# Two halves of a weight chunk in one PSUM bank in the mixers' products, and one eviction for both where nothing stands between them

## The chip, the cores and the metric

The kernel runs on one core of a Trainium2 chip. The time is the device time of one execution in microseconds; the runs are compared by their medians. The profile is of one execution, and names TensorE (PE, with its weight loads PEld), VectorE (DVE), ScalarE (ACT), GpSimd (POOL) and SyncE (SP, which issues most DMAs).

## The reference

It is one block with a gated delta mixer and 16 experts, and behind it a second block of two layers, all in float32 on 256 tokens of 1024 features. The change is in the second block only. Cut to what matters:

```python
def second_block(x, ...):
    for l in range(2):
        x = x + 0.5 * swiglu_ffn(rms_norm(x, g_ffn1[l]), w_up1[l], w_down1[l])
        h = rms_norm(x, g_mix[l])
        z = h @ w_in[l]            # lx, lg, q, k, v (1024 columns each), forget (16), gates (2048)
        xr = causal_depthwise_conv(z_lx, conv_w[l], conv_b[l])
        hr = rg_lru(xr, ...)       # gates by 128 x 128 blocks, then a scan along the tokens
        y_lru = (gelu(z_lg) * hr) @ w_lru_out[l]
        o = forgetting_attention(q, k, v, f_logit, ...)   # 16 heads of 64, q and k normed per head
        y_attn = o @ w_attn_out[l]
        m = gate_lru * y_lru + gate_attn * y_attn
        x = x + m @ w_o[l]
        x = x + 0.5 * swiglu_ffn(rms_norm(x, g_ffn2[l]), w_up2[l], w_down2[l])
    return x
```

## The kernel before

The first block takes the first half of the span. Behind it stands block2, with two layers of feed-forward, mixer, feed-forward. Features lie on the 128 partitions, the 256 tokens (T) along the rows, so that a product gives a tile of 128 x 256.

Products keep float32 accuracy: each operand is split into a high and a low part of a faster type, and three matmuls of 128 x 256 are summed for every 128 rows of the contraction (mm3, lines 235 to 237). With 8 such blocks a product is 24 matmuls. The activations are split once per norm (xh and xl, lines 248 and 249). Weights come in chunks of 128 x 2048: SyncE starts the DMA into a ring, ScalarE copies each half of the chunk into the high part (whi, line 222), VectorE subtracts for the low part (wlo, line 223). The function weights keeps two chunks split ahead, and there are four buffers each of whi and wlo. A chunk of the mixer feeds two products, one per half (u = 0, 1), or one per half of the tokens for v.

Each product goes into a PSUM bank of the pool "mm", which has three (bank, line 402); a bank holds 128 x 512 float32. Attention has its own banks, "s" (three) and "sm" (two).

The mixer (mix) runs four groups, g = 0 to 3, each a chunk of q, k, v and lx. queries evicts each q and k product by a multiplication with the norm's factor rstd (VectorE, line 527) and squares it on ScalarE (line 529); norms sums the squares with matmuls (line 537). values evicts v on ScalarE with the factor per token (line 551). recurrence evicts lx on VectorE (line 636), runs the short convolution (line 641) and appends two scans. Attention (lines 553 to 619) and the scans (line 651 and on) run in the background: they are generators in the list live, and project advances each of them by one step after a product (tick). The Tile scheduler then sets the final order on each engine. A scan's two matmuls share one "mm" bank, and each half is read by a tanh on ScalarE (line 653).

Behind the groups come four chunks of lg (line 681), the gates (their two products share a bank and have been evicted by one 128 x 512 operation, line 699), the two output branches (la, lines 710 to 722) and w_o: each of its eight products is added to x on VectorE (line 732), and after each the next norm takes its step (high part on ScalarE, low part xl on VectorE, square, sum on GpSimd). The norm's sums are then summed over partitions by one matmul (line 258).

Of the kernel before, what the change touches and what calls it, by code (L numbers as in the profile page):

```python
# [12 lines left out]
AF = mybir.ActivationFunctionType  # L13
ALU = mybir.AluOpType
AX = mybir.AxisListType
P = 128
# [145 lines left out]
def ks(t):  # L162
    return [t[:, k] for k in range(KD)]
# [6 lines left out]
class Kernel:  # L170
# [257 lines left out]
    def mix(self, l, x, norm):  # L428
        nc, d, wp, ps = self.nc, self.d, self.wp, self.ps
        with ExitStack() as es:  # L430
# [71 lines left out]
            def project(out, *args, f=self.proj):  # L502

                nonlocal rstd
                f(out, *args)
                if rstd is None:
                    rstd = finish()
                tick()

            live.append(tokens())  # L510
            tmp("gap", (P, GAP2))
# [6 lines left out]
            def queries(g):  # L518

                qk[g] = [tmp("qs", (P, 2, T), 1), tmp("kk", (P, 2, T), 1)]  # L520
                sqs = []
                for i, nm in enumerate(("w_q", "w_k")):
                    w = self.weights(nm, l * 4 + g)
                    for u in range(2):
                        pq = self.bank()
                        project(pq[:, :T], w, u, xh, xl)
                        nc.vector.tensor_mul(qk[g][i][:, u], pq[:, :T], rstd)  # L527
                        sqs.append(tmp("sq", (P, T), 4))
                        nc.scalar.activation(sqs[-1], qk[g][i][:, u], AF.Square)
                live.append(norms(sqs, g))  # L530
# [13 lines left out]
            def values(g):  # L544

                vt[g] = tmp("vt", (P, 2, T), 2)
                w = self.weights("w_v", l * 4 + g)
                for t in range(2):
                    pv = self.bank()
                    project(pv[:, :T], w, xh, xl, slice(t * P, (t + 1) * P), f=self.vproj)  # L550
                    nc.scalar.activation(vt[g][:, t], pv[:, :T], AF.Copy, scale=rc[:, t:t + 1])

# [71 lines left out]
            def recurrence(g):  # L624
# [3 lines left out]
                nc.sync.dma_start(wax, d["w_ax"][l * 4 + g])  # L628
                w = self.weights("w_lx", l * 4 + g)
                for u in range(2):  # L630
                    m = 2 * g + u
                    pq = self.bank()
                    project(pq[:, :T], w, u, xh, xl)
                    lx = tmp("lx", (P, T + 3), 2)
                    nc.gpsimd.memset(lx[:, :3], 0.0)
                    nc.vector.tensor_mul(lx[:, 3:], pq[:, :T], rstd)
                    cw = lambda j: self.c(f"conv_w{l}", j * KD + m)
# [38 lines left out]
            for g in range(4):  # L676
                w = self.weights("w_lg", l * 4 + g)
                for u in range(2):
                    pq = self.bank()
                    project(pq[:, :T], w, u, xh, xl)  # L680
                    nc.vector.tensor_mul(lg[:, 2 * g + u], pq[:, :T], rstd)
            for e in range(2):
# [9 lines left out]
            def gates(m):  # L692
# [4 lines left out]
                tg[m] = tmp("tg", (P, 2, T), TG)  # L697
                p2 = pq.rearrange("p (s n) -> p s n", s=2)
                nc.vector.tensor_mul(tg[m], p2, rstd[:, None, :].to_broadcast([P, 2, T]))
                for s in range(2):  # L700
# [25 lines left out]
            for c in range(4):  # L726
                w = self.weights("w_o", l * 4 + c)
                for u in range(2):
                    m = 2 * c + u
                    pq = self.bank()  # L730
                    self.proj(pq[:, :T], w, u, ks(mh), ks(ml))
                    nc.vector.tensor_add(x[:, m], pq[:, :T], x[:, m])
                    norm[2](m)
# [852 lines left out]
```

## Time and profile before

| | us |
|---|---|
| median of three runs | 2591.66 |
| the three runs | 2591.61, 2591.66, 2594.95 |
| the profiled execution | 2593.31 |
| its span | 2591.6 |
| TensorE busy | 2238.6 (86%) |
| VectorE busy | 1204.3 (46%) |
| ScalarE busy | 990.8 (38%) |
| GpSimd busy | 288.4 (11%) |
| mixer of layer 0 | about 1502 to 1778 |
| mixer of layer 1 | about 2137 to 2412 |

Times in a trace are counted from the start of the span. A row of the timeline gives an operation's start, its duration, its engine and line, the tile that it writes and those that it reads, and in square brackets how long its engine had been idle ahead of it and what ended that. Matmuls overlap in TensorE's pipe: their shown duration is longer than the distance of their starts, which is what counts in a row of them. VectorE and ScalarE begin an operation shortly before the one ahead is shown to end.

### The profile page before, as it was taken

The numbers are of one execution on the slowest core, as the hardware profiler recorded it, in microseconds if no ns is written. First come the engines' busy times: TensorE is split into PE (matmuls) and PEld (weight loads), VectorE is DVE, ScalarE is ACT, GpSimd is POOL, SyncE is SP. The second block draws the span as 40 slices with busy tenths as digits, with TensorE's granted clock in tenths as the row PEclk, the third lists the DMA queues.
The fourth block names the chain that finished last, engine by engine and source line by source line (L and its number), as shares of the span: only waits on it lengthen the run. The fifth ranks groups of instructions, "written<-read, shape, count | busy, mean of one in ns | idle before, by whom it ended". The sixth has DMA issues, their size and how long they took to land.

```text
span 2591.6 us, 40993 instructions
## 1 busy us (share of the span) xinstructions
PE 2238.6 (86%) x17204; PEld 1683.9 (65%) x17204; DVE 1204.3 (46%) x1924; ACT 990.8 (38%) x1619; POOL 288.4 (11%) x373
## 2 busy tenths in 40 slices
PE   7998997676677667666799999999999999999999
PEld 3666883111122111111189988999999998899999
DVE  4797751000000000000055679867566568986654
ACT  4674651000000000000055567645555556765553
POOL 2442000000000000000011121102111111111110
PEclk9999998878888887888789999999999999999999
DMA  6146259999999999999945543455555554345554
GB/s 256 69 176 212 82 232 384 430 431 429 431 430 430 430 431 429 431 429 431 429 181 196 195 145 135 161 188 188 196 195 184 193 204 146 123 163 196 185 193 144
DMA packets 75160, 681.24 MB, mean 263 GB/s; under 512 B 10080, under 2 KB 13792, under 8 KB 15072
## 3 DMA queue, kind: packets, MB, share of 16 engines
q1 hardware_dynamic: 71920, 677.48, 66.0%
q8 instruction: 135, 2.21, 0.3%
q10 hardware_dynamic: 3056, 1.15, 0.2%
q14 instruction: 49, 0.40, 0.0%
HBM read 677.47 MB, written 1.05 MB: 262 GB/s over the span
## 4 chain that ended last, share of the span: by engine, by line
PE 48%; DMA 35%; DVE 10%; ACT 4%; issue 2%; ACTq 0%; POOL 0%; SPq 0%; DVEq 0%; POOLq 0%
PE mm L235 13%; PE mm L236 13%; PE mm L237 13%; DMA arena<-e_down 10%; DMA arena<-e_up 7%; DMA arena<-e_gate 6%; DMA expert_ring<-e_gate 5%; DVE wlo L223 3%; DMA expert_ring<-e_down 3%; DMA ring<-e_up 1%; DMA ring<-e_down 1%; DMA early_zs<-w_mod 1%; DVE xr L641 1%; ACT whi L222 1%; DVE y L1128 1%
## 5 line engine op out<-in xcount | busy, mean ns | idle before, releaser
L223 DVE TENSOR_TENSOR wlo<-ring,whi 128x1024 fp32r<-128x1024 f32 x460 | 584.2, 1273 | 302.8 <-ACT whi L222 302.7
L222 ACT ACTIVATE whi<-ring 128x1024 fp32r<-128x1024 f32 x460 | 485.0, 1056 | 375.0 <-PE mm L236 334.3
L235 PE MATMUL mm<-xh,whi 128*128 128x256 f32 x2152 | 601.3, 280 | 10.6 <-DVE kk L527 7.1
L237 PE MATMUL mm<-xh,wlo 128*128 128x256 f32 x2152 | 599.4, 279 | 0.0
L236 PE MATMUL mm<-xl,whi 128*128 128x256 f32 x2152 | 598.1, 278 | 0.2
L235 PEld LDWEIGHTS mm<-xh,whi 128*128 128x128 f32 x2152 | 406.1, 189 | 15.5 <-issue 6.3
L237 PEld LDWEIGHTS mm<-xh,wlo 128*128 128x128 f32 x2152 | 405.9, 189 | 0.3
L236 PEld LDWEIGHTS mm<-xl,whi 128*128 128x128 f32 x2152 | 405.5, 188 | 0.9 <-DVE xl L249 0.6
L936 DVE TENSOR_TENSOR hid<-hid,u 128x512 f32<-128x512 f32 x16 | 11.0, 687 | 501.1 <-PE u L932 501.1
L235 PE MATMUL mm<-hh,whi 128*128 128x256 f32 x704 | 194.3, 276 | 0.0
L236 PE MATMUL mm<-hl,whi 128*128 128x256 f32 x704 | 194.3, 276 | 0.0
L237 PE MATMUL mm<-hh,wlo 128*128 128x256 f32 x704 | 194.3, 276 | 0.0
L932 PE MATMUL u<-arena,xs 128*32 128x512 f32 x608 | 108.3, 843 | 71.1 <-DMA arena<-e_up 71.1
L958 DVE COPY y<-x 128x512 f32<-128x512 f32 x16 | 11.1, 691 | 315.6 <-PE x L953 315.6
L236 PEld LDWEIGHTS mm<-hl,whi 128*128 128x128 f32 x704 | 132.2, 188 | 0.0
L235 PEld LDWEIGHTS mm<-hh,whi 128*128 128x128 f32 x704 | 132.2, 188 | 0.0
L237 PEld LDWEIGHTS mm<-hh,wlo 128*128 128x128 f32 x704 | 132.2, 188 | 0.0
L944 ACT ACTIVATE ht<-x 128x512 f32<-128x512 f32 x16 | 9.6, 597 | 304.4 <-PE x L942 304.4
L932 PEld LDWEIGHTS u<-arena,xs 128*32 128x32 f32 x608 | 19.7, 132 | 159.3 <-DMA arena<-e_up 123.0
L932 PE MATMUL g<-arena,xs 128*32 128x512 f32 x640 | 85.3, 660 | 40.3 <-DMA arena<-e_gate 40.3
L953 PE MATMUL d<-arena,ht 128*32 128x512 f32 x304 | 76.8, 787 | 48.9 <-DMA arena<-e_down 44.1
L957 ACT ACTIVATE y<-d 128x512 f32<-128x512 f32 x16 | 9.6, 597 | 279.9 <-PE d L953 279.9
(521 smaller groups left out, 3903.8 us busy)
## 6 DMA issues: line engine op xcount, KB each, us to landing
ring<-up SPq DMA_DIRECT2D x88, 1024.0 KB, 4.8
arena<-e_gate SPq DMA_DIRECT2D x40, 2048.0 KB, 34.4
arena<-e_up SPq DMA_DIRECT2D x38, 2048.0 KB, 35.1
arena<-e_down SPq DMA_DIRECT2D x38, 2048.0 KB, 34.2
ring<-down SPq DMA_DIRECT2D x44, 1024.0 KB, 4.8
expert_ring<-e_down SPq DMA_DIRECT2D x20, 2048.0 KB, 34.1
expert_ring<-e_up SPq DMA_DIRECT2D x19, 2048.0 KB, 34.1
expert_ring<-e_gate SPq DMA_DIRECT2D x18, 2048.0 KB, 34.0
```

The source lines that it names most:

```text
L222: nc.scalar.activation(hi, r, AF.Copy)
L223: nc.vector.tensor_sub(lo, r, hi.bitcast(F32))
L235: mm(out, ah, bh, start=start, stop=False)
L236: mm(out, ah, bl, start=False, stop=False)
L237: mm(out, al, bh, start=False, stop=stop)
L641: nc.vector.scalar_tensor_tensor(xr, lx[:, j:j + T], cw(j), xr, op0=ALU.mult, op1=ALU.add)
L932: nc.tensor.matmul(gu[s][32 * q:32 * q + 32], xs[:, k, ec], w[:, 512 * q:512 * q + 512], start=(k == 0), stop=(k == KD - 1))
L936: nc.vector.tensor_mul(hid, hid, gu[1])
L944: nc.scalar.activation(ht, xb, AF.Copy)
L953: nc.tensor.matmul(dn[n][32 * q:32 * q + 32], ht[:, i * P + 32 * q:i * P + 32 * q + 32], ws[q][:, o:o + 512], start=(i == 0), stop=(i == 3))
L958: nc.vector.tensor_copy(y[1], dn[1])
L1128: stt(yv[:, :, o], sv[:, :, i], cw(j), yv[:, :, o], op0=ALU.mult, op1=ALU.add)
```

## The change

The two products of a chunk go into the two halves of one "mm" bank. For q, k and lg one VectorE operation of 128 x 512 evicts both (scaled, with rstd broadcast over the halves), and for q and k one ScalarE operation squares both. For v, lx and w_o the halves share the bank, but each half is still evicted by an operation of its own. The gates had this form and now use the new function. The number of banks stays at three.

```diff
--- before.py
+++ after.py
@@ -507,6 +507,16 @@
                     rstd = finish()
                 tick()
 
+            def two(f, w):
+
+                pq = self.bank()
+                for u in range(2):
+                    f(pq[:, u * T:(u + 1) * T], w, u, xh, xl)
+                return pq
+
+            def scaled(out, pq):
+                nc.vector.tensor_mul(out, pq.rearrange("p (s n) -> p s n", s=2), rstd[:, None, :].to_broadcast([P, 2, T]))
+
             live.append(tokens())
             tmp("gap", (P, GAP2))
             hr, lg = big(0), big(1)
@@ -521,12 +531,11 @@
                 sqs = []
                 for i, nm in enumerate(("w_q", "w_k")):
                     w = self.weights(nm, l * 4 + g)
-                    for u in range(2):
-                        pq = self.bank()
-                        project(pq[:, :T], w, u, xh, xl)
-                        nc.vector.tensor_mul(qk[g][i][:, u], pq[:, :T], rstd)
-                        sqs.append(tmp("sq", (P, T), 4))
-                        nc.scalar.activation(sqs[-1], qk[g][i][:, u], AF.Square)
+                    pq = two(project, w)
+                    scaled(qk[g][i], pq)
+                    sq = tmp("sq", (P, 2, T), 2)
+                    nc.scalar.activation(sq, qk[g][i], AF.Square)
+                    sqs += [sq[:, u] for u in range(2)]
                 live.append(norms(sqs, g))
 
             def norms(sqs, g):
@@ -545,10 +554,11 @@
 
                 vt[g] = tmp("vt", (P, 2, T), 2)
                 w = self.weights("w_v", l * 4 + g)
+                pv = self.bank()
                 for t in range(2):
-                    pv = self.bank()
-                    project(pv[:, :T], w, xh, xl, slice(t * P, (t + 1) * P), f=self.vproj)
-                    nc.scalar.activation(vt[g][:, t], pv[:, :T], AF.Copy, scale=rc[:, t:t + 1])
+                    h = pv[:, t * T:(t + 1) * T]
+                    project(h, w, xh, xl, slice(t * P, (t + 1) * P), f=self.vproj)
+                    nc.scalar.activation(vt[g][:, t], h, AF.Copy, scale=rc[:, t:t + 1])
 
             def attention(g):
                 qz, kz = tmp("qz", (P, 4, T), 2), tmp("kz", (P, 4, T), 2)
@@ -627,13 +637,14 @@
                 wax = tmp("wax", (P, 512), 2)
                 nc.sync.dma_start(wax, d["w_ax"][l * 4 + g])
                 w = self.weights("w_lx", l * 4 + g)
+                pq = self.bank()
                 for u in range(2):
                     m = 2 * g + u
-                    pq = self.bank()
-                    project(pq[:, :T], w, u, xh, xl)
+                    h = pq[:, u * T:(u + 1) * T]
+                    project(h, w, u, xh, xl)
                     lx = tmp("lx", (P, T + 3), 2)
                     nc.gpsimd.memset(lx[:, :3], 0.0)
-                    nc.vector.tensor_mul(lx[:, 3:], pq[:, :T], rstd)
+                    nc.vector.tensor_mul(lx[:, 3:], h, rstd)
                     cw = lambda j: self.c(f"conv_w{l}", j * KD + m)
                     xr = lr[0][:, u]
                     nc.scalar.activation(xr, lx[:, 0:T], AF.Identity, bias=self.c(f"conv_b{l}", m), scale=cw(0))
@@ -675,10 +686,7 @@
             other = self.aside(xh, xl)
             for g in range(4):
                 w = self.weights("w_lg", l * 4 + g)
-                for u in range(2):
-                    pq = self.bank()
-                    project(pq[:, :T], w, u, xh, xl)
-                    nc.vector.tensor_mul(lg[:, 2 * g + u], pq[:, :T], rstd)
+                scaled(lg[:, 2 * g:2 * g + 2], two(project, w))
             for e in range(2):
                 r = slice(4 * e, 4 * e + 4)
                 nc.scalar.activation(lg[:, r], lg[:, r], AF.Gelu_apprx_tanh)
@@ -695,8 +703,7 @@
                 for s in range(2):
                     project(pq[:, s * T:(s + 1) * T], w, s, *((xh, xl) if m or s else other))
                 tg[m] = tmp("tg", (P, 2, T), TG)
-                p2 = pq.rearrange("p (s n) -> p s n", s=2)
-                nc.vector.tensor_mul(tg[m], p2, rstd[:, None, :].to_broadcast([P, 2, T]))
+                scaled(tg[m], pq)
                 for s in range(2):
                     nc.scalar.activation(tg[m][:, s], tg[m][:, s], AF.Tanh, scale=0.5,
                                          bias=hb[:, 8 * s + m:8 * s + m + 1])
@@ -725,11 +732,12 @@
             norm = self.norm(x, f"g_ffn2{l}")
             for c in range(4):
                 w = self.weights("w_o", l * 4 + c)
+                pq = self.bank()
                 for u in range(2):
                     m = 2 * c + u
-                    pq = self.bank()
-                    self.proj(pq[:, :T], w, u, ks(mh), ks(ml))
-                    nc.vector.tensor_add(x[:, m], pq[:, :T], x[:, m])
+                    h = pq[:, u * T:(u + 1) * T]
+                    self.proj(h, w, u, ks(mh), ks(ml))
+                    nc.vector.tensor_add(x[:, m], h, x[:, m])
                     norm[2](m)
             return norm
```

The scheduler tracks a bank as a whole, so the order around these products moves too. In the rows below an instruction's line stands first, then its operation, what it writes and reads, and the semaphores of the engines for which it waits; mm_ with a number is one PSUM bank's tile, whi and wlo are weight halves, xh and xl the split activations. The lines of the changed kernel are 8 to 11 further down for the same statements (651 becomes 662, 751 becomes 759, 610 becomes 620).

The first place is TensorE in group 2, where the first half of k ends and the second begins, with a matmul of the scan (line 651) between them. Before:

```order
L236 MATMUL mm_9558<-xl_7901,whi_9446 128x256
L237 MATMUL mm_9558<-xh_7900,wlo_9447 128x256
L651 MATMUL mm_9583<-xr_9322,wax_9325 128x256 [waits DVE_49]
L235 MATMUL mm_9601<-xh_7900,whi_9450 128x256 [waits DVE_49]
L236 MATMUL mm_9601<-xl_7901,whi_9450 128x256
```

After:

```order
L236 MATMUL mm_9534<-xl_7901,whi_9426 128x256
L237 MATMUL mm_9534<-xh_7900,wlo_9427 128x256
L662 MATMUL mm_9559<-xr_9303,wax_9306 128x256 [waits DVE_49,PE_49]
L235 MATMUL mm_9534<-xh_7900,whi_9430 128x256
L236 MATMUL mm_9534<-xl_7901,whi_9430 128x256
```

The second half of k had a bank of its own, for which it waited for VectorE; now it goes on in the bank of the first half and waits for nothing.

The second place is TensorE in group 1, at the scan's last matmul (line 651, into a bank that a tanh reads). Before, it stands in the second half of k:

```order
L235 MATMUL mm_9179<-xh_7900,whi_9028 128x256
L236 MATMUL mm_9179<-xl_7901,whi_9028 128x256
L651 MATMUL mm_9161<-xr_8919,wax_8922 128x256 [waits Activation_49]
L237 MATMUL mm_9179<-xh_7900,wlo_9029 128x256
L235 MATMUL mm_9179<-xh_7900,whi_9028 128x256
```

After, it stands behind the transposes of the attention (line 620) and the first matmul of v (line 759):

```order
L620 MATMUL sm_9192<-pack_base,p_1226_9000 128x128 [waits DVE_49]
L620 MATMUL sm_9192<-pack_base,p_1226_9000 128x128
L759 MATMUL mm_9212<-whi_9114,xh_7900 128x256 [waits Activation_49]
L662 MATMUL mm_9147<-xr_8910,wax_8913 128x256 [waits Activation_49]
L760 MATMUL mm_9212<-wlo_9115,xh_7900 128x256
```

Ten matmuls of k and the six transposes have moved ahead of it. In groups 2 and 3 the same pair of places is found after, while before it stood between transposes or in k.

The third place is TensorE in w_o of layer 0, at the end of the first half of its first chunk; b_ are the two parts of the mixed branches. Before, the second half follows at once in another bank:

```order
L237 MATMUL mm_11694<-b_1486_10647,wlo_11618 128x256
L235 MATMUL mm_11694<-b_1486_10647,whi_11617 128x256 [waits Activation_49]
L236 MATMUL mm_11694<-b_1487_10648,whi_11617 128x256 [waits DVE_49]
L237 MATMUL mm_11694<-b_1486_10647,wlo_11618 128x256
L235 MATMUL mm_11723<-b_1486_10647,whi_11621 128x256
L236 MATMUL mm_11723<-b_1487_10648,whi_11621 128x256
```

After:

```order
L235 MATMUL mm_11646<-b_1458_10599,whi_11569 128x256 [waits Activation_49]
L236 MATMUL mm_11646<-b_1459_10600,whi_11569 128x256 [waits DVE_49]
L237 MATMUL mm_11646<-b_1458_10599,wlo_11570 128x256
L235 MATMUL mm_11715<-b_1458_10599,whi_11638 128x256
L236 MATMUL mm_11715<-b_1459_10600,whi_11638 128x256
L237 MATMUL mm_11715<-b_1458_10599,wlo_11639 128x256
L235 MATMUL mm_11715<-b_1458_10599,whi_11638 128x256
L236 MATMUL mm_11715<-b_1459_10600,whi_11638 128x256
L235 MATMUL mm_11646<-b_1458_10599,whi_11573 128x256 [waits DVE_49]
L236 MATMUL mm_11646<-b_1459_10600,whi_11573 128x256
```

Five matmuls of the second chunk (mm_11715) now stand between the halves of the first, whose second half waits for VectorE. Further on the same is done with seven matmuls of the next chunk ahead of each second half.

## Rows read from the trace of the kernel before

**Rows 1.** The page: TensorE's busy time; the chain that ended last, by engine.

```profile
PE 2238.6 (86%) x17204; PEld 1683.9 (65%) x17204; DVE 1204.3 (46%) x1924; ACT 990.8 (38%) x1619; POOL 288.4 (11%) x373
PE 48%; DMA 35%; DVE 10%; ACT 4%; issue 2%; ACTq 0%; POOL 0%; SPq 0%; DVEq 0%; POOLq 0%
```

**Rows 2.** Stretches: length, busy PE, PEld, DVE, ACT, POOL, then clock, DMA share, GB/s.

```profile
1545.00:1578.00 33.00, 32.09 (x265) 30.05 (x264) 32.28 (x62) 23.34 (x50) 5.96 (x11) 1.00 0.41 139
...
1664.00:1752.00 88.00, 87.81 (x774) 87.58 (x773) 60.70 (x67) 44.76 (x58) 8.70 (x10) 1.00 0.55 192
```

**Rows 3.** TensorE's waits, 1502 to 1778: us in total, times, longest.

```profile
PE mm L235 <- DVE kk L527: 3.5, 2, 2.6
PE ss L258 <- POOL sums L253: 1.3, 2, 0.9
PE mm L235 <- ACT ti L653: 0.9, 1, 0.9
...
PE mm L651 <- DVE qs L527: 0.4, 1, 0.4
```

**Rows 4.** Timeline of TensorE in w_o: two matmuls in a row.

```profile
1753.08 0.28 PE L235 MATMUL mm<-b,whi 128*128 128x256 f32 x1
1753.19 0.28 PE L236 MATMUL mm<-b,whi 128*128 128x256 f32 x1
```

**Rows 5.** Two lines' durations: ns min/median/max, first and last start, forms.

```profile
L527 DVE TENSOR_TENSOR kk<-mm,rstd x16: 404/419/425, 1514.5 to 2249.7; 128x256 f32<-128x256 f32 x16
...
L699 DVE TENSOR_TENSOR tg<-mm,rstd x16: 677/692/692, 1668.0 to 2367.5; 128x512 f32<-128x512 f32 x16
```

**Rows 6.** Timeline in group 1: a matmul into a bank being read.

```profile
1540.17 0.48 ACT L653 ACTIVATE th<-mm,hb 128x256 f32<-128x256 f32 x1
...
1540.70 0.30 PEld L651 LDWEIGHTS mm<-xr,wax 128*128 128x128 f32 x2 [0.16 <-ACT th L653]
```

**Rows 7.** Timeline in group 3: TensorE's longest wait in the mixer.

```profile
1608.13 2.35 DVE L223 TENSOR_TENSOR wlo<-ring,whi 128x1024 fp32r<-128x1024 f32 x2
...
1610.40 0.41 DVE L527 TENSOR_TENSOR kk<-mm,rstd 128x256 f32<-128x256 f32 x1
...
1610.96 0.36 PE L235 MATMUL mm<-xh,whi 128*128 128x256 f32 x1 [2.57 <-DVE kk L527]
```

**Rows 8.** Timeline of TensorE: where group cycles begin, and one wait.

```profile
1548.19 0.36 PE L751 MATMUL mm<-whi,xh 128*128 128x256 f32 x1
...
1575.49 0.60 PE L651 MATMUL mm<-xr,wax 128*128 128x256 f32 x2
1577.00 0.38 PE L235 MATMUL mm<-xh,whi 128*128 128x256 f32 x1 [0.91 <-DVE kk L527]
...
1580.86 0.36 PE L751 MATMUL mm<-whi,xh 128*128 128x256 f32 x1
...
1615.41 0.36 PE L751 MATMUL mm<-whi,xh 128*128 128x256 f32 x1
...
1648.05 0.37 PE L235 MATMUL mm<-xh,whi 128*128 128x256 f32 x1
```

**Rows 9.** Timeline in group 1: the scan's last matmul; the next low halves.

```profile
1545.99 0.42 PE L651 MATMUL mm<-xr,wax 128*128 128x256 f32 x1
...
1557.48 2.28 DVE L223 TENSOR_TENSOR wlo<-ring,whi 128x1024 fp32r<-128x1024 f32 x2
```

**Rows 10.** Timeline of ScalarE at the mixer's start: issues of DMAs.

```profile
1518.81 2.52 ACTq L563 DMA_DIRECT2D qz<-cum  x4
```

**Rows 11.** Timeline of ScalarE and VectorE in w_o, one turn.

```profile
1755.55 1.06 ACT L222 ACTIVATE whi<-ring 128x1024 fp32r<-128x1024 f32 x1 [0.66 <-PE mm L236]
...
1756.64 1.22 DVE L223 TENSOR_TENSOR wlo<-ring,whi 128x1024 fp32r<-128x1024 f32 x1 [0.56 <-ACT whi L222]
...
1757.79 0.96 DVE L249 SCALAR_TENSOR_TENSOR xl<-x,pack_base,xh 128x256 fp32r<-128x256 f32 x1
...
1758.67 0.41 DVE L732 TENSOR_TENSOR x<-mm,x 128x256 f32<-128x256 f32 x1
```

## The prediction, made before the changed kernel was run

> **What bounds the kernel now.** I read the page's busy table and its chain of waits first, then busy time by stretches, then what TensorE waited for, then the timeline around each wait. The busy table and the chain [rows 1] show TensorE busy for 86% of the span, and the chain split between TensorE (48%) and DMA (35%). The DMA part is the expert weights of the first block, which the change does not touch. The change sits in the mixer of the second block, which runs twice: about 1502 to 1778 us and 2137 to 2412 us, with the same pattern both times. So every sum below is for one mixer and is doubled at the end.
>
> Inside a mixer the reader is to see two kinds of stretch [rows 2]. In the four groups (queries, values, recurrence, with attention in the background) TensorE is busy 32.09 of 33 us, but VectorE too, 32.28 of 33. Here the two engines run neck and neck. Behind the groups (gates, output branches) TensorE is busy 87.81 of 88 us and VectorE 60.70: TensorE alone sets the pace. A product is 24 matmuls at a pitch of 0.113 us (1753.08 to 1753.19) [rows 4], 2.72 us, and 96 of them take 10.85 us.
>
> What TensorE waited for in the whole mixer is little [rows 3]: 3.5 us for evictions of k (two waits, one of 2.6), 0.9 for ti (a tanh that reads a bank of the recurrence), 0.4 for q, 1.3 for the norm's sums. But for the last these are waits for one of the three "mm" banks to come free. The largest of them is plain in the timeline [rows 7]: a pair of weight splits holds VectorE from 1608.13, the eviction of k starts behind it at 1610.40, and TensorE starts the next product at 1610.96, 2.57 us late. The starts of the values of groups 1 to 3 and of the first product behind them [rows 8] give group cycles of 32.67, 34.55 and 32.64 us, 99.86 together. In the first one the pair at 1575.49 is followed only at 1577.00; its second matmul starts at 1575.71, and where nothing is late the next one follows 0.03 behind, so 1.26 is lost. A cycle without bank waits is thus 32.67 - 1.26 = 31.4 us. All bank waits of the three cycles are 99.86 - 94.2 = 5.7 us: that is the most that the change can win there.
>
> **Part 1: one eviction for two products (q, k, lg).** An eviction of 128x256 takes 0.41 us, one of 128x512 takes 0.69 (the gates' own, which has this very form) [rows 5]. So two become one, 2 x 0.41 - 0.69 = 0.13 us less on VectorE, 12 times in a mixer: 1.6 us of VectorE time. Behind the groups this is hidden under TensorE; it counts in the group cycles only, as slack. What counts is that the second half of a chunk now writes the bank that the first half already holds: it needs no free bank, so the wait of [rows 7] has no place there any more. The price is that the first half's eviction now waits for the second half.
>
> **Part 2: the group cycles.** To the 31.4 I add three things. First, 0.2: the scheduler now cuts v, lx and the next q into pieces that alternate with the attention's matmuls in other places, with one more change of operand type. Second, 0.15: the second half of v and of lx writes the bank that the first half's eviction reads. The trace has such a case: the pair at L651 goes into a bank that a tanh reads until 1540.65, and its weight load, 0.16 idle for that tanh, starts at 1540.70, 0.05 behind its end [rows 6]. For v the order puts 19 matmuls of lx between the halves, for lx 14 of the next q, so only a part is left. Third, the next group's q needs its low weight half. The order puts the last matmul of the recurrence's scan behind the first one of v; before, in group 1, it came earlier, in k, at 1545.99. The low half of the next q began at 1557.48 on VectorE as one of two that take 2.28 together [rows 9], so it was ready at 1558.62, 12.6 us later, long before q came at its old place behind lx. Now q's first 14 matmuls stand ahead of the second half of lx, and between the scan's last matmul and q's third are 23 of v, 19 of lx, 24 of v, 5 of lx and 2 of q: 73 at 0.113, 8.25 us. The rest of a cycle, 31.4 less eight products of 2.72, is 9.6 us of attention and scan matmuls; a good quarter of them lies between, 2.6 by my estimate: 10.85 us. I take 11.5 for the chain: 12.6 less the eviction of k and its square (0.41 + 0.40), which now come ahead of it, and 0.3 for the queueing between them, an estimate. That leaves a wait of 0.65 us per cycle; its bounds are 0 (the chain is done in 10.85) and 2.0 (12.6 and 0.28 for the longer eviction in front). The sum is 31.4 + 0.2 + 0.15 + 0.65 = 32.4 per cycle, 97.2 for three, against 99.86: **2.7 us won**, with bounds from 4.8 won (31.7 per cycle, most of the 0.15 hidden, no wait) to 1.4 lost (33.75).
>
> **Part 3: the mixer's start.** On ScalarE the one square of k (128x512) now stands behind four DMA issues, which held the queue 2.52 us in the trace [rows 10], and behind a split, and the table load of the norms stands behind it again. The norms' matmuls come later for it, and v's second half waits for the first's eviction behind them on ScalarE: some 2.4 us in all. The old waits in group 1 (0.9 for ti, 0.4 for q [rows 3], and the steps around them, 1.9 in all against the pitch) go with it: a start that is later meets VectorE and ScalarE further on. So I set 2.4 against 1.9, and **0.5 us is lost**, between 0 and the whole 2.4.
>
> **Part 4: w_o.** Its halves share a bank but are still added to x one by one. VectorE's order is a fixed triple there, split, xl, add; the trace shows one turn of it [rows 11]: ScalarE's split from 1755.55 for 1.06, VectorE's from 1756.64 for 1.22, xl from 1757.79 for 0.96, add from 1758.67 to 1759.08. The product before had ended at 1755.40 (ScalarE's split waited for TensorE, by its row, and started 0.15 behind). So an add ends 3.7 us after the end of the product before its own, and TensorE can go on then. Before the change nobody waited for it: the next product had its own bank. Now the second half of a chunk waits. The scheduler puts 7 matmuls of the next chunk ahead of it: from the end of the product before, TensorE has 19 + 7 = 26 matmuls, 2.95 us, less the 0.15 by which it had begun: 2.8. The wait is 3.7 - 2.8 = 0.9 us for each of chunks 1 to 3, 2.7 together. Chunk 0 adds 0.1 (five matmuls, 0.57, ahead of an eviction of 0.41 and two handovers), and the next block's norm sum adds 0.4, since 18 matmuls cover it now instead of 22. **3.2 us lost.** The bounds: 0.5 if the xl takes 0.48 (as it does when POOL is still) and the scheduler's cover holds, so that only the last two terms are left, and 4.4 if another eviction of 0.41 stands in front each time.
>
> A page speaks against the change. The Trainium skill, "Perfetto Trace Analysis", section "Matmuls", says that independent matmul groups should go round different PSUM banks, so that the evacuation of one runs beside the matmuls of the next. This trace agrees in one place only [rows 6]; how far it bears on the halves is the third rival's matter.
>
> **The sum.** Per mixer 0.5 - 2.7 + 3.2 = +1.0 us, for two +2.0. The profiled execution took 2593.3 us (span 2591.6, and 1.7 around it), which becomes 2595.3; it stands 1.65 above the median of three runs, 2591.66. On the median's scale I predict **2593.7 us**. With a measurement that can tell about 0.2%, 5.2 us, from no change, this is no change.
>
> **The rivals.**
> - The cover is enough everywhere: cycles of 31.7 (4.8 won), w_o at its low bound (0.5), the start free. That is 4.3 won per mixer, 2583.1 us. For it: the scheduler did put cover in each place, and VectorE has 1.6 us more slack. Against: VectorE's 32.28 of 33 us, and the fixed triple of w_o. Chance 0.15.
> - Slower: the split queue comes late. One mechanism, in the group cycles: the low half of the next q's weights, behind the scan on VectorE. From 12.6 us after the scan's second half on, instead of my 11.5, the wait is 2.0 and the cycles 33.75, 1.4 lost; with 0.5 and 3.2 this is 5.1 per mixer, 2601.9 us. For it: VectorE is full there and the chain did take 12.6 before. Against: it has less in it now. Chance 0.18.
> - The halves are serialised through their bank: every second half of v, lx and w_o, 12 in a mixer, waits for the whole eviction of the first: 0.28 for the last matmul to end, 0.42 to 0.48 for the eviction and 0.08 of handovers, less the 0.11 of a pitch, 0.7 each, 8.2 in all. With the bank waits gone (and part of the rest hidden) 4.0 are lost per mixer, 2599.8 us. This is the result that the page's rule leads to. Against: the order has background or other products' matmuls between halves in most places. Chance 0.03.
> - The change does not do what it says: the bank waits stay, because VectorE is late and not the banks short. Then nothing of the 2.7 is won, the lost 0.5 and 3.2 remain, 3.7 per mixer, 2599.1 us. Against: in [rows 7] the eviction comes late, and a second half that needs no bank would have passed it. Chance 0.07.
>
> **How the numbers follow.** My forecast has 0.57, and holds what ends within 5.2 us. Faster by over 0.2% is the first rival, 0.15; slower by over 0.2% the other three, 0.28; within 0.2% 0.57. The slower side reaches to 2601.9, the faster to 2583.1. To leave no more than 2 in 10 out, the range goes from 2585 to 2602: it leaves out the first rival and a little above. The forecast alone would be 2587 to 2597.
>
> **What the trace after would show.** TensorE's wait for evictions of k, 3.5 us before, should be near 0. Group cycles of about 32.4 speak for part 2; 33.5 and more, with TensorE waiting for a low weight half at q, for the second rival; 31.7 for the first. In w_o TensorE should wait three times some 0.9 us for the add to x; no waits there would make part 4 wrong, and the time about 5 us shorter. The norms' matmuls of group 0 should wait for the square of k. The fused evictions should take 0.69. What would make it wrong altogether is a wait of more than 1 us in the groups that I have not named, or VectorE falling further behind from group to group.

## The result

The changed kernel took 2606.18 us (median of four runs, 2601.12 to 2609.97), the kernel before, measured beside it, 2591.64 (2590.16 to 2594.95): a ratio of 1.0053, with a 95% interval of 1.0041 to 1.0065. So it is slower by 0.5%, some 14 us, where 2 us were forecast; the time lies above the range of 2585 to 2602. The profiled execution took 2609.97 us, its span 2608.2.

To see where the time went I compare the stretches of the two profiles between the same matmuls of TensorE. The first norm sum of layer 0's mixer (line 258) starts at 1504.4 us before and at 1508.0 after. The 3.6 us ahead of it lie in code that the change does not touch, and this start differs from one execution to the next: over the fourteen profiles of this case it lies between 1496.5 and 1508.0. From there to the end of the span it is 1087.2 us before and 1100.2 after: 13.0 us more, which is about what the runs say. I use this second part below as the stretch from the first norm sum on. It is one execution per kernel; its two layers agree to 0.1 or 0.2 us in most rows, and by 1.5 us where the clock fell (last section).

| us, layer 0 / layer 1 | before | after | difference |
|---|---|---|---|
| first norm sum to v of group 1 | 43.77 / 43.93 | 43.22 / 44.70 | -0.55 / +0.77 |
| v of group 1 to v of group 2 | 32.67 / 32.74 | 33.63 / 33.66 | +0.97 / +0.92 |
| v of group 2 to v of group 3 | 34.56 / 34.64 | 33.63 / 33.72 | -0.93 / -0.92 |
| v of group 3 to the first gate's product | 46.41 / 46.32 | 49.92 / 50.06 | +3.51 / +3.74 |
| first gate's product to the second norm sum | 113.00 / 113.00 | 117.05 / 117.11 | +4.05 / +4.11 |
| the next feed-forward | 181.30 / 182.20 | 180.47 / 180.86 | -0.83 / -1.34 |

(Between layer 0's next feed-forward and layer 1's mixer lies one more feed-forward, 182.63 before and 182.11 after.) The next three groups of rows are of the profile after. The starts of the group cycles on TensorE's timeline (start, duration), the place eight products behind the last of them, where the prediction's third cycle ends, and the first gate's product, which reads ah:

```profile
1551.27 0.36 PE L759 MATMUL mm<-whi,xh 128*128 128x256 f32 x1
...
1584.90 0.36 PE L759 MATMUL mm<-whi,xh 128*128 128x256 f32 x1
...
1618.54 0.36 PE L759 MATMUL mm<-whi,xh 128*128 128x256 f32 x1
...
1653.89 0.37 PE L235 MATMUL mm<-xh,whi 128*128 128x256 f32 x1
...
1668.46 0.38 PE L235 MATMUL mm<-ah,whi 128*128 128x256 f32 x1
```

They answer [rows 8]: the first two cycles now take 33.63 us each and the third 35.35, against 32.67, 34.55 and 32.64. The cycle that was long before is shorter, and the two short ones are longer. What TensorE waited for in the whole mixer (us in total, times, longest), which answers [rows 3]:

```profile
PE mm L237 <- DVE wlo L223: 3.3, 3, 1.3
PE sm L546 <- ACT sq L537: 1.9, 1, 1.9
PE mm L235 <- DVE x L740: 1.7, 3, 0.6
PE ss L258 <- POOL sums L253: 1.5, 2, 0.9
```

No eviction of k or q is in the list any more (3.5 and 0.4 before), nor the tanh ti (0.9). In their place stand three waits for a low weight half, one for the square of k, and three for the addition to x. Busy time by stretches (length, PE, PEld, DVE, ACT, POOL, clock, DMA share, GB/s), which answers [rows 2]:

```profile
1551.00:1585.00 34.00, 33.02 (x266) 30.40 (x265) 30.47 (x54) 23.50 (x48) 5.99 (x11) 1.00 0.36 126
...
1680.00:1755.00 75.00, 75.00 (x664) 75.00 (x663) 49.15 (x56) 37.93 (x49) 5.16 (x7) 1.00 0.54 192
```

VectorE is less full in the groups: 30.47 of 34 us, where it was 32.28 of 33. The stretch of before was its fullest, though. Over the two cycles from v of group 1 to v of group 3, before and after (length and busy time in total, then the mean of the two):

```profile
sum 67.22, PE 63.73 PEld 59.49 DVE 62.23 ACT 46.91 POOL 7.79; mean PE 31.87 PEld 29.75 DVE 31.12 ACT 23.45 POOL 3.90
sum 67.27, PE 65.31 PEld 60.07 DVE 60.60 ACT 46.27 POOL 7.82; mean PE 32.65 PEld 30.04 DVE 30.30 ACT 23.14 POOL 3.91
```

VectorE works 1.6 us less in the same time. Four fused evictions, 0.13 us each, are 0.5 of that; the rest was not taken apart. TensorE shows as busy as ever, which hides part of the loss: its rows are as many, but they stand further apart.

### The profile page after: what moved, and what is told of

Read it like the earlier page. It is cut to its first block, busy times and chain, and to the rows that moved or that the text cites. A ratio compares the mean times of both kernels' runs of the same rounds, so it can differ in the third digit from the quotient of the medians.

```text
span 2608.2 us, 40951 instructions
## 1 busy us (share of the span) xinstructions
PE 2236.7 (86%) x17204; PEld 1686.4 (65%) x17204; DVE 1199.9 (46%) x1896; ACT 988.2 (38%) x1607; POOL 289.2 (11%) x373
## 4 chain that ended last, share of the span: by engine, by line
PE 53%; DMA 34%; DVE 7%; ACT 3%; issue 2%; POOL 1%; ACTq 0%; SPq 0%; DVEq 0%; POOLq 0%
PE mm L235 14%; PE mm L237 14%; PE mm L236 14%; DMA arena<-e_down 8%; DMA arena<-e_gate 6%; DMA arena<-e_up 6%; DMA expert_ring<-e_gate 5%; DMA ring<-e_up 3%; DMA expert_ring<-e_down 3%; DVE wlo L223 1%; DMA ring<-e_down 1%; DMA expert_ring<-e_up 1%; DMA early_zs<-w_mod 1%; ACT whi L222 1%; DVE tt L1312 1%
## 5 line engine op out<-in xcount | busy, mean ns | idle before, releaser
L223 DVE TENSOR_TENSOR wlo<-ring,whi 128x1024 fp32r<-128x1024 f32 x460 | 576.0, 1256 | 307.1 <-ACT whi L222 304.6
L357 POOL TENSOR_TENSOR hl<-hid,hh 128x256 fp32r<-128x256 f32 x88 | 68.4, 777 | 427.1 <-ACT hh L356 427.1
L943 ACT ACTIVATE hid<-g 128x512 f32<-128x512 f32 x16 | 9.6, 597 | 276.3 <-PE g L940 276.3
```

What stands on the lines that cost most here:

```text
L223: nc.vector.tensor_sub(lo, r, hi.bitcast(F32))
L357: nc.gpsimd.tensor_sub(hl[:, m], hid, hh[:, m].bitcast(F32))
L943: nc.scalar.activation(hid, gu[0], AF.Silu)
```

## Where the time goes in the group cycles

The first new wait, in group 1's cycle: the scan's last matmuls, the low half of the next q, and q's third matmul on the timeline.

```profile
1551.47 0.59 PE L662 MATMUL mm<-xr,wax 128*128 128x256 f32 x2
...
1562.24 0.37 PE L235 MATMUL mm<-xh,whi 128*128 128x256 f32 x1
1562.44 0.28 PE L236 MATMUL mm<-xl,whi 128*128 128x256 f32 x1
1562.44 1.19 DVE L223 TENSOR_TENSOR wlo<-ring,whi 128x1024 fp32r<-128x1024 f32 x1
...
1563.69 0.38 PE L237 MATMUL mm<-xh,wlo 128*128 128x256 f32 x1 [0.97 <-DVE wlo L223]
```

The second of the pair starts at about 1551.69. The low half is ready at 1563.63, 11.9 us later; TensorE was there at 1562.55, 10.9 us later. It loses 1.13 us against the pitch. The same happens in each cycle, and in the last one, where the next product is of lg, the loss is 1.48.

The second part is no wait at all. The order now puts the second half of lx into the middle of the attention's last matmuls (lines 628 and 629; 618 and 619 before). The kernel before, the kernel after:

```profile
1561.51 0.28 PE L237 MATMUL mm<-xh,wlo 128*128 128x256 f32 x1
1561.71 0.66 PE L618 MATMUL s<-pts,vt 128*64 128x256 f32 x4
1562.19 0.39 PE L619 MATMUL s<-pts,vt 128*64 128x128 f32 x4
1562.52 1.21 PE L571 MATMUL s<-rn,selt 128*128 128x256 f32 x8
```

```profile
1565.06 0.28 PE L236 MATMUL mm<-xl,whi 128*128 128x256 f32 x1
1565.27 0.65 PE L628 MATMUL s<-pts,vt 128*64 128x256 f32 x2
1565.84 0.39 PE L235 MATMUL mm<-xh,whi 128*128 128x256 f32 x1
...
1568.57 0.28 PE L237 MATMUL mm<-xh,wlo 128*128 128x256 f32 x1
1568.78 0.32 PE L629 MATMUL s<-pts,vt 128*64 128x128 f32 x1
1568.79 0.43 PE L628 MATMUL s<-pts,vt 128*64 128x256 f32 x1
1568.94 0.27 PE L629 MATMUL s<-pts,vt 128*64 128x128 f32 x1
1569.05 0.38 PE L628 MATMUL s<-pts,vt 128*64 128x256 f32 x1
1569.27 0.38 PE L629 MATMUL s<-pts,vt 128*64 128x128 f32 x2
1569.58 0.39 PE L581 MATMUL s<-rn,selt 128*128 128x256 f32 x1
```

Before, these matmuls stand in one piece, 1.01 us from the last product's matmul to the next kind. After, they are in two pieces of 0.78 and 1.01 us: each change from a product to them or back takes 0.2 to 0.3 us from start to start instead of the 0.11 of a pitch, and so does a step from the first of their two forms to the second (0.20 on average, 12 such steps now and 8 before). From v of group 1 to the first gate's product I sorted TensorE's steps from one matmul's start to the next: steps over 0.45 us (what exceeds a pitch of 0.12) are the waits, the rest is the pace. Before: 5.1 us of waits and 108.5 of pace, 50 changes between products and other matmuls. After: 4.5 of waits and 112.7 of pace, 62 changes. So **the bank waits are gone, waits of another kind and nearly the same length stand in their place, and 4.2 us more go into the pace**. Of the 4.2, 3.5 are steps into, within and out of the attention's last matmuls, 0.7 the scan's pair that now cuts v. No run keeps the shared banks and the old order of these matmuls, so this part rests on the steps of the trace. The number of changes alone is not the price, as a kernel below (lx's bank, two evictions) has 60 of them and a pace of 110.5.

## The experiments

All ratios are against the kernel before on the same chip, with 95% intervals; in brackets, of one profiled execution each, the stretch from the first norm sum on, 1087.2 us before and 1100.2 after. Differences in microseconds follow from the ratio. First the parts of the change apart.

**Fused evictions alone.** v, lx and w_o as before; q, k, lg as after (the edit is against the changed kernel):

```diff
-                pv = self.bank()
                 for t in range(2):
-                    h = pv[:, t * T:(t + 1) * T]
+                    h = self.bank()[:, :T]
...
-                pq = self.bank()
                 for u in range(2):
                     m = 2 * g + u
-                    h = pq[:, u * T:(u + 1) * T]
+                    h = self.bank()[:, :T]
```

(and the same in w_o). 

> Only the fused evictions of q, k and lg are kept; v, lx and w_o have a bank for each half again. Theory A (the loss is the shared banks with two evictions: w_o waits for the add to x, and sharing lx draws the next q ahead of its low weight half): the bank waits of the group cycles go and nothing is added, cycles of 31.4 to 31.8 us, some 4 us won per mixer, 8 in all, about 2583. Theory B (the loss is the fused eviction, which comes only after both halves and makes norms and the next steps late): cycles stay at 33 or more, time at 2594 or above.

Measured: 0.9986 (0.9975 to 0.9996), 3.6 us faster (1085.4, of which some 1.2 are a stretch at half clock, 0.50 in the rows of the last section, in layer 0). The sign is that of theory A, the size half of it. The cycles of groups 1 and 2 are 33.41 and 31.66. The waits of the whole mixer show why, and below them ScalarE and TensorE at the longest one:

```profile
PE mm L660 <- ACT th L662: 2.8, 2, 1.6
PE sm L546 <- ACT sq L537: 1.9, 1, 1.9
```

```profile
1575.56 0.50 ACT L607 ACTIVATE p<-s,nm 128x256 f32<-128x256 f32 x1
1576.01 0.88 ACT L662 ACTIVATE th<-mm,hb 128x256 f32<-128x256 f32 x2
1576.57 0.48 PE L660 MATMUL mm<-xr,wax 128*128 128x256 f32 x1 [1.63 <-ACT th L662]
```

The bank waits are gone, but the scan's matmuls now meet the tanh ahead of them on ScalarE, which stands behind attention's exponentials (line 607). Theory B failed, as the time is below 2594; of the later eviction what shows is the wait of 1.9 us for the square of k.

**w_o alone.** Only w_o shares its bank (the edit is against the kernel before):

```diff
+                pq = self.bank()
                 for u in range(2):
                     m = 2 * c + u
-                    pq = self.bank()
-                    self.proj(pq[:, :T], w, u, ks(mh), ks(ml))
-                    nc.vector.tensor_add(x[:, m], pq[:, :T], x[:, m])
+                    h = pq[:, u * T:(u + 1) * T]
+                    self.proj(h, w, u, ks(mh), ks(ml))
+                    nc.vector.tensor_add(x[:, m], h, x[:, m])
```

> Only w_o shares a bank. Theory A: three waits for the add to x in each mixer, 0.74 each above the pitch, and the norm sum 0.2 to 0.4 later; 3.2 per mixer less what moves into the next block, 5 to 6.5 us in all, about 2598; the group cycles as before (32.7, 34.6, 32.6). Theory B: the waits at w_o are paid back in the next block, whose weights come earlier, and the time stays within 2 us of before.

Measured: 1.0019 (1.0009 to 1.0029), 4.9 us slower (1095.4). The stretch from the first gate's product to the second norm sum is 4.00 and 4.12 us longer, and the next feed-forward gives 1.33 and 0.81 back: 6 us in all, as theory A had it. The other 2 us of the bracket are something else: the cycle of group 2, with the old bank wait at its end, took 36.1 to 36.2 us in both layers instead of 34.6, because of the clock (last section).

**v and lx alone**, with two evictions each; q, k, lg and w_o as before. 

> Only v and lx share banks. Theory A: the next q starts ahead of the second half of lx and waits 1.1 us or more for its low weight half in each cycle, and there are more changes between matmul types; cycles of 33.6 or more, 3 to 8 us slower in all, about 2597. Theory B: the bank waits at k go partly, since v and lx take fewer banks, and nothing else changes: 2588 to 2592.

Measured: 1.0021 (1.0011 to 1.0030), 5.4 us slower (1094.9). The waits for the low half are there (3.5 us in a mixer), the cycles 34.4 and 34.2 to 34.3: theory A. Here a product of v also waits 1.1 us for v's eviction on ScalarE.

**All but w_o.** 

> All of the change but w_o. Theory A: the change less its w_o part, 13.7 - 6.5 = 7 us slower than before, about 2599, with cycles of 33.6 as in the changed kernel. Theory B: 2605, as the whole change, since w_o gives back what it loses.

Measured: 1.0018 (1.0009 to 1.0026), 4.7 us slower (1093.1), where 7 were forecast, cycles 33.69 and 33.74, waits for the low half 2.9 us: theory A. Against the fused evictions alone, the two shared banks cost 7.7 us by the bracket and 8.3 by the two ratios.

Next, which of the two, and why. **Fused evictions and v's bank.** 

> The fused evictions of q, k, lg and the shared bank of v; lx and w_o with a bank for each half. Theory C (of the two shared banks it is lx that costs: its second half waits for VectorE, so the order draws 14 matmuls of the next q ahead of it, and these meet their low weight half too late): no wait for the low half at q, time from the first norm sum on as with the fused evictions alone, 1085 to 1087 us. Theory D (v's bank costs as much, by its wait for the eviction on ScalarE): 1089 or more.

**Fused evictions and lx's bank.** 

> The fused evictions and the shared bank of lx; v and w_o with a bank for each half. Theory C: three waits of 1 us or more for the low half in each mixer, 1091 to 1094 us from the first norm sum on, 5 to 8 us slower than with the fused evictions alone. Theory D: 1087 to 1089.

Measured: with v 1.0001 (0.9993 to 1.0010; 1089.8, of which some 3 are two stretches at half clock), with lx 1.0004 (0.9995 to 1.0012; 1086.5). The waits of a whole mixer, first the kernel with v's bank, then that with lx's:

```profile
PE mm L661 <- ACT th L663: 2.1, 3, 1.2
...
PE mm L661 <- DVE b L518: 0.9, 1, 0.9
```

```profile
PE mm L237 <- DVE wlo L223: 3.0, 3, 1.2
```

Theory C is right in its mechanism: the wait for the low half comes with lx's bank and only with it. Its time for lx's bank, 1091 to 1094, was missed, and it is wrong in saying that v's bank costs nothing. From v of group 1 to the first gate, fused evictions alone take 112.33 us, with v's bank 113.58, with lx's 113.97, with both (all but w_o) 117.46. Each costs little and both together 5.1: the pace is 108.8 us with neither, 110.0 with v's, 110.5 with lx's and 113.3 with both. In this stretch both together cost 2.2 us more than the sum, most of it in the pace; why was not taken further apart. The times of the whole program do not show it: against the fused evictions alone the ratios stand 0.0015 higher with v's bank, 0.0018 with lx's and 0.0032 with both, each uncertain by some 0.0013.

**lx fused as well.** One eviction for both halves of lx; v and w_o with a bank for each half (the edit is against the fused evictions alone):

```diff
+                lx2 = tmp("lx", (P, 2, T + 3), 1)
+                nc.gpsimd.memset(lx2[:, :, :3], 0.0)
+                scaled(lx2[:, :, 3:], two(project, w))
                 for u in range(2):
                     m = 2 * g + u
-                    h = self.bank()[:, :T]
-                    project(h, w, u, xh, xl)
-                    lx = tmp("lx", (P, T + 3), 2)
-                    nc.gpsimd.memset(lx[:, :3], 0.0)
-                    nc.vector.tensor_mul(lx[:, 3:], h, rstd)
+                    lx = lx2[:, u]
```

> The fused evictions of q, k, lg, and lx in one bank too but evicted by one 128x512 operation; v and w_o with a bank for each half. Theory C: with no eviction between the halves nothing has to be drawn ahead, q stays behind lx, and no wait for the low half is left: 1082 to 1087 us from the first norm sum on. Theory D (a shared bank costs in itself): 1090 or more.

Measured: 0.9994 (0.9985 to 1.0003; 1085.4). No wait for the low half is left, and the changes between kinds fall to 48: by the bracket lx's shared bank costs nothing by itself, only the eviction between its halves does. The ratio is as near to that with lx's bank and two evictions (1.0004) as to that of the fused evictions alone, so here the waits decide and not the time. The scan's waits for the tanh are 4.2 us here, since both scans now start together.

**w_o with one addition** of 128x512 for both halves, all else as before (the edit is against the kernel before):

```diff
+                pq = self.bank()
                 for u in range(2):
-                    m = 2 * c + u
-                    pq = self.bank()
-                    self.proj(pq[:, :T], w, u, ks(mh), ks(ml))
-                    nc.vector.tensor_add(x[:, m], pq[:, :T], x[:, m])
-                    norm[2](m)
+                    self.proj(pq[:, u * T:(u + 1) * T], w, u, ks(mh), ks(ml))
+                xc = x[:, 2 * c:2 * c + 2]
+                nc.vector.tensor_add(xc, pq.rearrange("p (s n) -> p s n", s=2), xc)
+                for u in range(2):
+                    norm[2](2 * c + u)
```

> Only w_o shares a bank, and one 128x512 addition takes both halves into x; all else as before the change. If the wait of w_o is for the addition between the halves (my reading), the three waits of 0.74 us go, and only the last chunk's norm steps come later, by 1 to 2 us ahead of the norm sum: 0.5 to 2 us per mixer, 2593 to 2596. If sharing the bank costs in itself, 2598 as with w_o shared and two additions.

Measured: 1.0000 (0.9991 to 1.0008; 1089.5, with two stretches at half clock). The three waits for x are gone. The norm sum comes 4.3 us later, and the next feed-forward gives back all of it but 0.3 (177.26 instead of 181.30), since its matmuls now stand ahead of the sum. So w_o's loss is the addition between the halves.

Last, what limits the fused evictions. **DMAs on SyncE.** On top of the fused evictions alone. The rows of cum for attention were issued on ScalarE:

```diff
-                            nc.scalar.dma_start(zz[r + row:r + row + 1, u, s], (cum, ncum)[i][h:h + 1])
+                            nc.sync.dma_start(zz[r + row:r + row + 1, u, s], (cum, ncum)[i][h:h + 1])
```

> The fused evictions of q, k, lg alone, and the rows of cum for attention are fetched by DMAs issued on SyncE in place of ScalarE. If the wait of the norm sums at the mixer's start (1.9 us for the fused square of k) comes from the DMA issues ahead of that square on ScalarE, it falls to under 0.5 us, the start is 1.5 us shorter per mixer, and the stretch at half clock behind it goes too: 1080 to 1083 us from the first norm sum on, against 1085.3. If it comes from the square itself (it needs both halves of k), the wait stays at 1.5 us or more and the time does not change.

Measured: 0.9988 (0.9978 to 0.9999; 1086.1). The wait at the start did fall, from 1.9 to 0.7 us, so it was for the DMA issues in the main; but the order moved elsewhere (the cycle of group 2 went from 31.66 to 33.61), and the time is the same. The forecast time was missed.

**The scans one product earlier**, on top of that:

```diff
-WAIT = (3, 2, 2, 2, 1, 2, 1)
+WAIT = (3, 2, 2, 2, 1, 1, 1)
```

> As the run before, and the scans start one product earlier. If the waits of the scan's matmuls for a tanh (2.8 us in a mixer with the fused evictions alone) come from the exponentials of attention that stand ahead of that tanh on ScalarE, an earlier scan meets ScalarE ahead of them and these waits fall to under 1 us: cycles of 31.4 to 32, 4 us less over both mixers than the run before, 1076 to 1080 us. If ScalarE is late whatever stands there, nothing changes or weights come later: 1081 or more.

Measured: 0.9995 (0.9983 to 1.0008; 1090.4). The waits for the tanh are gone, but one of 2.1 us for an attention copy on VectorE has come, with a stretch at half clock behind it. The kernel leaves the engine of these copies open (nc.any), and with this order 30 of the 32 copies are on VectorE, against 16 in the run ahead. A miss: the wait was moved to another engine, and the run changed more than the place of the scans.

**lx fused and the scans earlier**, without and with the DMAs on SyncE. 

> Fused evictions of q, k, lg and lx, and the scans one product earlier; DMAs on ScalarE as before. The waits of the scan's matmuls for a tanh (4.2 us with lx fused) should fall to about 1 us: 1080 to 1083 us from the first norm sum on, with the wait of 1.9 us at the start left. If they stay, 1085.

> As the run before with the DMAs issued on SyncE: another 1.5 us less per mixer if the start's wait is for the DMA issues, 1077 to 1080 us; else as the run before.

Measured: 0.9988 (0.9978 to 0.9997; 1084.9, with one stretch at half clock) and **0.9966 (0.9953 to 0.9978; 1080.0)**. The first missed its 1080 to 1083 and the second met 1077 to 1080; the waits for the tanh fell from 4.2 us to 1.8, not to 1. The latter, 2584.24 us (median of five runs), is by its ratio 8.8 us faster than the kernel before. The waits of its whole mixer:

```profile
PE mm L659 <- ACT th L661: 1.8, 3, 0.6
PE ss L258 <- POOL sums L253: 1.3, 2, 0.9
PE sm L546 <- ACT sq L537: 0.7, 1, 0.7
```

From v of group 1 to the first gate it takes 111.4 us, 1.5 of waits and 109.9 of pace, against 113.6 before.

## Why the prediction was wrong, by its own steps

- *The sum and its sign.* +1.0 us per mixer was forecast, +6.2 and +7.3 measured (stretches of the table added up, of the second 1.5 by the clock; the feed-forward between the layers gives 0.5 back). Almost all of the difference is in part 2.
- *Part 1, the durations:* right. The fused evictions take 0.66 to 0.69, and VectorE has more slack in the groups.
- *Part 2, the group cycles:* this step failed. The bank waits went, as said; the stretch's 5.1 us were close to the 5.7. What was added was mis-sized. The wait for the low half was put at 0.65 per cycle and was 1.13, and 1.48 in the last one: the chain took 11.9 us, where I took 11.5 between 10.85 and 12.9. The larger error is the 0.2 for the products cut in another place and the 0.15 for v and lx. A cycle of 33.63 less the wait of 1.13 is 32.5, against the 31.4 of a cycle without waits: 1.1 instead of 0.35. I had counted one more change of operand type per cycle, and the order shows twelve more from v of group 1 to the gates; the duration of each stands in the trace of before (1561.51 to 1561.71, 0.20) and I did not multiply. The 0.2 was worked out from no row. I took the third cycle to be like the other two, but it is the worst, 35.35 us for the forecast 32.4: lg's own product is drawn ahead in it, its wait is the longest, and the attention's last matmuls stand in two pieces there too. The prediction's three cycles together were to win 2.7 us and lost 2.8; up to the first gate's product the loss is 3.5 to 3.7.
- *Part 3, the start:* the wait for the square of k came, 1.9 us, from the place named. But the old waits of group 1 went altogether, and layer 0 won 0.55 where 0.5 was to be lost. In layer 1 it cost 0.77, but without the 1.5 of the clock it would have won some 0.7 there too. The sign of the 0.5 was wrong.
- *Part 4, w_o:* right, in mechanism and size. One turn of VectorE and TensorE's wait behind it, after (answers [rows 11]):

```profile
1770.60 1.23 DVE L223 TENSOR_TENSOR wlo<-ring,whi 128x1024 fp32r<-128x1024 f32 x1 [0.56 <-ACT whi L222]
1771.74 0.96 DVE L249 SCALAR_TENSOR_TENSOR xl<-x,pack_base,xh 128x256 fp32r<-128x256 f32 x1
1772.63 0.41 DVE L740 TENSOR_TENSOR x<-mm,x 128x256 f32<-128x256 f32 x1
...
1773.10 0.39 PE L235 MATMUL mm<-b,whi 128*128 128x256 f32 x1 [0.57 <-DVE x L740]
```

  Against the pitch each of the three costs 0.73, and the step behind it 0.11 more (forecast 0.9). Chunk 0 costs 0.2 and the norm sum 0.4, which makes 3.2, as forecast. The table's 4.05 is longer by 0.8, for seven matmuls of the next feed-forward that now stand ahead of the norm sum; the feed-forward gives 0.8 to 1.3 back, so the net loss is 2.8 to 3.2 us per mixer.
- *The rivals.* The second, the slower one, named one of the two mechanisms that the trace shows: the low half that comes late behind the scan. It was priced as a wait of 2.0 us per cycle, 1.4 lost in three; the waits were smaller (1.13, 1.13 and 1.48), and the cut matmuls, which no rival had, more than made up for it. In the changed kernel the third rival's 0.7 for each half held for w_o only. The page that speaks for it, the Trainium skill's "Perfetto Trace Analysis", section "Matmuls", advises to rotate independent groups through banks so that an evacuation runs beside the next group. The trace agrees for w_o (0.57 idle for each addition), and the runs with one eviction for both halves show where it ends: with nothing that reads a shared bank between its two groups, no wait for that eviction is left (w_o with one addition 1.0000).
- *The range.* Its upper end was the second rival's sum, 5.1 us per mixer, with 1.4 lost in the group cycles. The 3.5 to 3.7 measured there up to the gates, and the clock, lie beyond it.

## What to carry to other kernels

Here sharing a bank between two products left no wait for it when one operation evicted both, and cost when each half had its own: this scheduler holds the dependency for the whole bank, and fills the hole with work that was to come later and whose inputs are late. When an order changes, count the changes between kinds of matmul in it and multiply each kind by what it takes in the trace; they appear in no list of waits. A wait that is removed on a full engine can turn up at the next one (here from VectorE's eviction to ScalarE's tanh), and here the time followed only when several places had been mended at once.

## What the runs showed of the hardware

A wait of about 2 us on TensorE was followed in some executions by some 3 us at half clock, and in others by none. In layer 1 of the changed kernel, TensorE at the mixer's start (stretches as above; the figure behind the POOL column is the granted clock), and the wait on its timeline:

```profile
2163.00:2166.00 3.00, 1.18 (x10) 0.29 (x8) 1.38 (x2) 1.57 (x2) 0.00 (x0) 1.00 0.03 2
2166.00:2169.00 3.00, 3.00 (x15) 2.92 (x14) 0.95 (x2) 2.12 (x3) 0.00 (x0) 0.50 0.50 159
2169.00:2172.00 3.00, 3.00 (x27) 3.00 (x26) 1.15 (x2) 1.40 (x3) 0.00 (x0) 0.93 0.48 189
```

```profile
2165.51 0.64 PE L546 MATMUL sm<-sq,pack_block 128*32 128x256 f32 x4 [1.82 <-ACT sq L537]
2166.08 0.58 PE L235 MATMUL mm<-xh,whi 128*128 128x256 f32 x1
2166.46 0.42 PE L236 MATMUL mm<-xl,whi 128*128 128x256 f32 x1
2166.68 0.41 PE L237 MATMUL mm<-xh,wlo 128*128 128x256 f32 x1
```

The clock falls to 0.50, the lower of its two levels (1.2 of 2.4 GHz), matmuls follow at 0.21 instead of 0.113, and the stretch is 1.5 us longer than in layer 0, where the same wait of 1.9 us left the clock at 1.00. With w_o alone shared, the bank wait of 2.6 us in group 2's cycle was followed by 0.50 in both layers (36.1 us); in the profile of the kernel before the same wait left 1.00 (34.6). Over all fourteen profiles TensorE has 22 waits of 1.8 to 2.7 us in the mixers, and 11 of them are followed so; no other stretch of the mixers is at 0.50. What decides between the two was not found. It makes a wait of 2 us worth up to 3.5, and profiles of one execution each can differ by that.
